# Relative bias tables: one slot and 32 writes, one per step, in place of three slots and 48 writes

## The chip, the cores and the metric

The kernel runs on one core of a Trainium2 chip. The time is device microseconds of one execution; before the change the median of three runs is 1170.31 us (1169.25 to 1171.8). The engines are named as in the profile: PE (TensorE matmul), PEld (its weight load), DVE (VectorE), ACT (ScalarE), POOL (GpSimd) and SP (the queue that issues most DMAs).

## What is computed

A two-layer encoder on 512 tokens (a grid of 8 rows and 64 columns) of width 1024, all in float32. Layer 0 is two kinds of global attention side by side, layer 1 a neighbourhood attention, and each is followed by a squared-ReLU MLP; a norm ends it. The change touches the bias of the neighbourhood attention, and the MLP of layer 0, beside which the bias is prepared:

```python
rs = jnp.clip(qr - wr // 2, 0, rows - wr)          # 8 rows of 8: always 0
cs = jnp.clip(qc - wc // 2, 0, GRID_W - wc)        # first of 16 columns
kr = rs[:, None, None] + jnp.arange(wr, dtype=jnp.int32)[None, :, None]
kc = cs[:, None, None] + jnp.arange(wc, dtype=jnp.int32)[None, None, :]
ridx = jnp.broadcast_to(kr - qr[:, None, None] + (C_WIN_ROWS - 1), (s, wr, wc)).reshape(s, -1)
cidx = jnp.broadcast_to(kc - qc[:, None, None] + (C_WIN_COLS - 1), (s, wr, wc)).reshape(s, -1)
...
bias = rpb[:, rblk, cblk].astype(jnp.float32)
sc = jnp.einsum('bhqd,bhqkd->bhqk', qblk, kg).astype(jnp.float32) * scale + bias[None]
...
def sq_relu_mlp(h, w_up, w_down):
    u = jax.nn.relu(h @ w_up)
    return (u * u) @ w_down
```

`rpb` has 16 heads, 15 row distances and 31 column distances.

## The kernel before

**Products in three passes.** Every float32 factor is split into a high part (fp32r, made by ACT) and a low part (the rest, made by DVE), and each product is three matmuls: high by high, high by low, low by high. `mm3` (L603 to L606) issues them for 512 columns, `Seven.run` (L448 to L450) for 256: the latter computes a 2 x 2 block product with seven products in place of eight, on sums of weight blocks that POOL forms (`seven_chunk`, L356 to L358) before ACT (L362, tile `whi`) and DVE (L363, tile `wlo`) split them.

**Memory.** SBUF holds 32 equal slots of 128 x 1024 floats. `Slot()` takes the one that has been free longest, `free()` puts it at the end of the list; whoever takes a slot waits for its last readers, DMAs included. Weights pass through `raw` (4 buffers), `whi` (3) and `wlo` (4).

**The second product of the MLP (`mlp(0)`).** It has three parts. First `product8` (L521 to L562): eight chunks of 128 rows of `ffn_w_down`, 512 KB each, against eight PSUM banks (s, t, t, o, mm, mm, mm, s), in 64 steps of three matmuls; the chunks k = 0 and 1 run first over four banks, then over the other four, k = 2 to 5 one after the other, and the last two bank by bank, so that DVE can add each bank into `hT` (L1536) as it is finished. From its third chunk on the low part of the weights is not made by DVE: SP loads the raw chunk (L252), ACT writes its negated high part to `wlo` (L255), a DMA that POOL issues (L256) adds the weights to it, and ACT makes the high part (L259). Second, beside these steps, `convert` splits the activations of the next product: ACT L417 and DVE L418, with DVE L390, L393 and L422 for the sums; each chunk takes new slots. Third, `u7.run` uses them, with weights of `seven_chunk` (SP L352). At its start another split takes two slots (ACT L964, DVE L961).

**The bias tables (`bias_rows`, L1472 to L1498).** For 16 column positions c within the window, and two kinds t of key sets (t = 0 for queries whose window lies inside, t = 1 for the tokens at the ends, whose other half is -1e30), the DRAM tensor `bx` receives a 128-row table of 256 values. Eight small DMAs (L1476) bring the bias, shifted by query row, into slot R; POOL fills slots Fi and Fe with -1e30 (L1479, L1480) and copies R into them (L1482, L1483); then SP writes, for each c, 128 KB from Fi (L1488), 64 KB from Fe (L1492) and 64 KB of -1e30 from Fe (L1494). It is a generator: `mlp` calls `next(bias)` twice per step of `product8` (L1560, L1561). In program order the writes fall on steps 7 to 30 of 64.

**The order on each engine.** A scheduler builds the rows of the engines from the program; what is marked `keep_in_program_order` stays in order, other work may be pulled forward. Each engine then runs its row in order. SP's DMAs use eight semaphores in turn, and each waits for the one eight places ahead.

**The reader.** In the neighbourhood attention each of the 16 heads loads its table from `bx` (L1789, 256 KB, two buffers `bias`), and DVE adds it to the scores (L1726). The same two buffers serve as split activations of the sixth chunk of `product8`.

Of the kernel before, what the change touches and what calls it, by code (L numbers as in the profile page):

```python
# [8 lines left out]
F32 = mybir.dt.float32  # L9
# [9 lines left out]
P = 128  # L19
# [3 lines left out]
NEG = -1e30  # L23
# [12 lines left out]
def encoder_kernel(ctx: ExitStack, tc: tile.TileContext, ins, out, dbg=None):  # L36
    nc = tc.nc
    PE, ACT, DVE, POOL, SP = nc.tensor, nc.scalar, nc.vector, nc.gpsimd, nc.sync
# [7 lines left out]
    dr = ctx.enter_context(tc.tile_pool(name="dr", bufs=1, space=bass.MemoryType.DRAM))  # L46
# [14 lines left out]
    def nm(s):  # L61
        cnt[0] += 1
        return f"{s}_{cnt[0]}"
# [271 lines left out]
    def finish_off():  # L335
        while off_d or off_a:
            catch_up()
# [30 lines left out]
    class Seven:  # L368
# [29 lines left out]
        def split(self, kp, held=lambda z: z):  # L398

            for b in range(7):  # L400
                i = self.number(kp, b) // 2
                if i not in self.slots:
                    self.slots[i] = Slot()
            raw, t = self.raw.pop(kp)
            own = isinstance(t, Slot)
            r, t_ = (s_.rearrange("p (b n) -> p b n", n=256) for s_ in (raw.t, t.t if own else t))

            T4 = t_[:, 2:3] if own else r[:, 3:4]
            src = lambda b, n: (r[:, 1 + b : 1 + b + n] if b < 3 else t_[:, b - 3 : b - 3 + n] if b < 5
                                else r[:, 0:1] if b == 5 else T4)  # L410
            b = 0
            while b < 7:
                q = self.number(kp, b)
                n = 2 if b == 3 or (b < 2 and q % 2 == 0) or (b == 5 and not own) else 1
                d = self.slots[q // 2].t.rearrange("p (q z n) -> p q z n", q=2, z=2)[:, q % 2 : q % 2 + n]
                s_ = r[:, 0:4:3] if b == 5 and n == 2 else src(b, n)
                ACT.activation(d[:, :, 0], s_, AF.Copy)  # L417
                held(DVE.tensor_tensor(d[:, :, 1], s_, f32(d[:, :, 0]), op=ALU.subtract))  # L418
                b += n
                yield  # L420
                if b == 3 and not own:
                    held(DVE.tensor_tensor(r[:, 3], r[:, 3], r[:, 0], op=ALU.subtract))  # L422
                    yield
            raw.free()
            if own:
                t.free()
# [140 lines left out]
    def tiles(c0, n):  # L567
        return [(c0 + o, min(P, n - o)) for o in range(0, n, P)]
# [5 lines left out]
    class Fill:  # L574
# [8 lines left out]
        def step(self):  # L583
            try:
                self.credit -= next(self.q[0][1])
            except StopIteration:
                self.q.pop(0)
# [879 lines left out]
        return stage, ahead, later  # L1467


    bx = dr.tile([16, 2, P, 256], F32, name="bx")  # L1470

    def bias_rows():  # L1472
        R, Fi, Fe = Slot(F32), Slot(F32), Slot(F32)
        rpb = ins["od_rpb"][0]
        for qr in range(8):
            SP.dma_start(R.t[16 * qr : 16 * qr + 16, 0:248],  # L1476
                           rpb.rearrange("h a b -> h (a b)")[:, (7 - qr) * 31 : (7 - qr) * 31 + 248])
            yield
        POOL.memset(Fi.t[:, 0:376], NEG)  # L1479
        POOL.memset(Fe.t[:, 256:512], NEG)  # L1480
        rv = R.t[:, 0:248].rearrange("p (k d) -> p d k", d=31)
        POOL.tensor_copy(Fi.t[:, 0:376].rearrange("p (j k) -> p j k", k=8)[:, 15:31, :], rv[:, 7:23, :])  # L1482
        POOL.tensor_copy(Fe.t[:, 0:248].rearrange("p (j k) -> p j k", k=8), rv)  # L1483
        for _ in range(6):
            yield
        bxv = bx.rearrange("h t (c r) k -> t c r h k", r=8)
        for c in range(16):
            SP.dma_start(bxv[0, c].rearrange("r h k -> r h k"), Fi.t[:, (15 - c) * 8 : (15 - c) * 8 + 256])  # L1488
            yield

            v, off = (1, (7 - c) * 8) if c < 8 else (0, (23 - c) * 8)
            SP.dma_start(bxv[1, c][:, :, 128 * v : 128 * v + 128], Fe.t[:, off : off + 128])  # L1492
            yield
            SP.dma_start(bxv[1, c][:, :, 128 - 128 * v : 256 - 128 * v], Fe.t[:, 256:384])  # L1494
            yield
        for s_ in (R, Fi, Fe):
            s_.free()
        yield  # L1498

    def convert(u7, R):  # L1500
        held = tc.keep_in_program_order
        for kp, raw in enumerate(R):
            yield from u7.sums(kp, raw, DVE, held)
            yield
            yield from u7.split(kp, held)

    def mlp(l, last=None):

        stage, ahead, later = first_product(l)
        reserve[0] = 3
        w = ins["ffn_w_down"][l]
        up4, gens4 = [], []

        def plain_last(k0, V):
            left = list(V)
            gens4.extend(product(w, k0, up4, tiles(512 * c, 512), lambda j, b, c=c: ev(4 * c + j, b), nk=2 * len(V))
                         for c in range(2))  # L1520

            def beside(m, i):
                if m == 0 and i % 8 == 4 and left:
                    w_ = left.pop(0)
                    for z in range(2):
                        U4.append(Slot())
                        up4.append(U4[-1].pair())
                        split(w_.t[:, S * z : S * z + S], up4[-1])
                    w_.free()

            return beside

        U4 = []

        def ev(m, b):
            return DVE.tensor_tensor(hT[:, m, :], hT[:, m, :], b, op=ALU.add)  # L1536

        U, _, _, (at_u, _), _ = stage(SIZES[l][0])
        up = [s_.pair() for s_ in U]
        gens = [product(w, at_u, up, tiles(512 * c, 512), lambda j, b, c=c: ev(4 * c + j, b)) for c in range(2)]  # L1540
        ahead()
        for c, gen in enumerate(gens):
            for i, _ in enumerate(gen):
                later(c, i)
        for s_ in U:
            s_.free()
        U, R, V, (at_u, at_r), late = stage(*SIZES[l][1:])
        first = [k + z for k in at_u for z in range(2)]
        gen = product8(w, first, U, ev)
        u7 = Seven(2 * len(R))  # L1550
        ids = [u7.plan(w, 256 * m, at_r) for m in range(4)]
        k0 = 32 - 2 * len(V)
        beside = (last or plain_last)(k0, V)
        bias = iter(()) if last else bias_rows()
        reserve[0] = NSLOT
        work, at = convert(u7, R), 0
        for i, _ in enumerate(gen):
            if i in (1, 4, 6):
                next(late, None)
            next(bias, None)  # L1560
            next(bias, None)  # L1561

            at += 9 * len(R) + 2
            while at > 0:
                next(work, None)
                at -= 8 * len(U) - 2
        for x in (work, bias):
            for _ in x:
                pass
        reserve[0] = 3  # L1570
        for m in range(4):

            def evac(w_):
                h2 = hT[:, 2 * m : 2 * m + 2, :]
                DVE.tensor_tensor(h2, h2, w_.t.rearrange("p (z n) -> p z n", z=2), op=ALU.add)

            for i, _ in enumerate(u7.run(ids[m], evac)):
                beside(m, i)
        u7.free()
        for gen in gens4:  # L1580
            for _ in gen:
                pass
        for s_ in U4:
            s_.free()
# [112 lines left out]
    def attend_C(step):  # L1697
# [45 lines left out]
        def weigh(w):  # L1743
            for p, tt in w:
                ACT.activation(p, p, AF.Exp, bias=tt[:, 0:1], scale=-1.0, accum_out=tt[:, 1:2])
# [35 lines left out]
        for n in range(16):  # L1781
            t, e = n // 2, n % 2
            if e == 0:
                fill.until(f"c{t}")
                finish_off()
            step(n)
            h = dict(d=PC[t], e=e, n=n)
            h["bias"] = scp.tile([P, 2, 256], F32, tag="bias", bufs=2, name=nm("bias"))
            SP.dma_start(h["bias"], bx[n].rearrange("t q k -> q t k"))  # L1789
            w = scores(h, (3, 0))  # L1790
            if prev:
                prev["pt"] = Slot(), Slot()
                turn(prev, *T1, w)
            else:
                weigh(w)
            rest(w, RATE_C - 0.15, ripe)
            w = scores(h, (1, 2))
            h["d"]["K"][e].free()
            if e:
                h["d"]["Q"].free()  # L1800
            if prev:
                turn(prev, *T2, w)
            else:
                weigh(w)
            rest(w, RATE_C + 0.15, None)
            prev, ripe = h, prev
# [265 lines left out]
```

## Time and profile before

| | |
|---|---|
| median of three runs | 1170.31 us (1169.25 to 1171.8) |
| profiled execution | 1171.35 us, its span 1169.6 us, mean granted clock 0.995 |
| PE, PEld busy | 98%, 88% |
| DVE, ACT, POOL busy | 76%, 57%, 51% |
| DMA | 134.37 MB, 115 GB/s |
| `product8` of layer 0 | 452 to 498 us of the span |

Times in the rows are microseconds from the span's start. A timeline row gives start, duration, engine, line, operation, output and input tiles, and in brackets how long the engine had been idle and what ended that. A row of windows gives a stretch, its length, the busy time of PE, PEld, DVE, ACT and POOL with the number of instructions, the granted TensorE clock (1.00 is full), the mean busy share of the core's 16 DMA engines, and GB/s. A row of a tile gives line, engine, operation, count, shortest, median and longest duration in ns, and the first and last start. Matmuls overlap, so their pace is read from their starts, not from their durations.

### The profile page before, as it was taken

What the parts mean: (1) busy time and instruction counts of PE and PEld (TensorE: products, weight loads), DVE (VectorE), ACT (ScalarE), POOL (GpSimd) and SP (SyncE); (2) the same over time, 40 slices, a digit from 0 to 9 for tenths busy, and PEclk for the clock granted to TensorE, in tenths of its full rate; (3) what the DMA queues carried; (4) which work ended last, traced back from release to release, by engine and by line L of the source; (5) the groups of instructions that cost most, each with busy time, mean ns of one, the idle gap of its engine ahead of it and who ended that gap; (6) DMA issues with size and microseconds to landing.
All of it is one profiled execution on the core that took longest, in us unless ns stands there. A gap on an engine that the chain in (4) does not pass through costs nothing.

```text
span 1169.6 us, 20581 instructions
## 1 busy us (share of the span) xinstructions
PE 1150.6 (98%) x7348; PEld 1025.9 (88%) x7348; DVE 892.6 (76%) x1544; ACT 668.4 (57%) x1135; POOL 602.0 (51%) x744
## 2 busy tenths in 40 slices
PE   9999999999999999989999999999999999999997
PEld 8787888887899999789987998988889999989996
DVE  6887988878868876676695676767997787688765
ACT  6676876756256658533453555655552666773445
POOL 4456252207687991279802232221288799526960
PEclk9999999999999999989999999999999999999999
DMA  7322314222523326823446564434343233282432
GB/s 234 108 75 66 96 59 131 64 84 91 168 77 88 100 73 180 221 82 100 127 127 160 135 176 133 125 102 136 99 148 105 83 99 99 60 202 64 127 118 72
DMA packets 115478, 134.37 MB, mean 115 GB/s; under 512 B 9667, under 2 KB 96880, under 8 KB 115376
## 3 DMA queue, kind: packets, MB, share of 16 engines
q1 hardware_dynamic: 111024, 120.09, 35.0%
q0 software_dynamic: 4032, 12.60, 5.5%
q8 instruction: 58, 0.95, 0.3%
q14 instruction: 44, 0.36, 0.1%
q10 hardware_dynamic: 320, 0.36, 0.1%
HBM read 110.61 MB, written 6.29 MB: 100 GB/s over the span
## 4 chain that ended last, share of the span: by engine, by line
PE 75%; DVE 7%; POOL 5%; DMA 4%; issue 4%; ACT 2%; SPq 2%; DVEq 0%; POOLq 0%; ACTq 0%
PE mm L604 8%; PE mm L605 8%; PE mm L606 8%; PE s L1128 3%; PE mm L450 3%; PE mm L448 3%; PE mm L449 3%; PE o L1116 3%; PE t L1103 2%; PE s L606 2%; PE s L604 2%; POOL raw L358 2%; PE s L605 2%; PE t L448 2%; PE t L450 2%
## 5 line engine op out<-in xcount | busy, mean ns | idle before, releaser
L604 PE MATMUL mm<-a,whi 128*128 128x512 f32 x428 | 173.8, 407 | 0.2
L363 DVE TENSOR_TENSOR wlo<-a,whi 128x896 fp32r<-128x896 f32 x103 | 130.1, 1266 | 53.8 <-ACT whi L362 53.5
L606 PE MATMUL mm<-a,wlo 128*128 128x512 f32 x428 | 168.9, 396 | 0.0
L605 PE MATMUL mm<-a,whi 128*128 128x512 f32 x428 | 168.9, 395 | 0.0
L362 ACT ACTIVATE whi<-a 128x896 fp32r<-128x896 f32 x103 | 97.5, 949 | 103.3 <-PE o L605 22.9
L233 ACT ACTIVATE whi<-raw 128x1024 fp32r<-128x1024 f32 (+3 forms) x100 | 92.2, 924 | 66.9 <-PE s L605 24.3
L223 DVE TENSOR_TENSOR wlo<-raw,whi 128x1024 fp32r<-128x1024 f32 (+4 forms) x97 | 110.0, 1138 | 25.1 <-ACT whi L233 20.8
L450 PE MATMUL mm<-a,wlo 128*128 128x256 f32 x430 | 120.7, 281 | 1.3 <-DVE wlo L363 1.2
L448 PE MATMUL mm<-a,whi 128*128 128x256 f32 x430 | 120.7, 281 | 0.0
L449 PE MATMUL mm<-a,whi 128*128 128x256 f32 x430 | 120.4, 280 | 0.0
L363 DVE TENSOR_TENSOR wlo<-raw,whi 128x896 fp32r<-128x896 f32 x61 | 72.8, 1197 | 49.8 <-ACT whi L362 49.5
L362 ACT ACTIVATE whi<-raw 128x896 fp32r<-128x896 f32 x61 | 57.9, 952 | 87.0 <-POOL raw L358 52.7
L358 POOL TENSOR_TENSOR a<-a 128x128 f32<-128x128 f32 x103 | 98.5, 956 | 8.1
L357 POOL TENSOR_TENSOR a<-a 128x256 f32<-128x256 f32 x103 | 94.9, 921 | 8.1
L606 PEld LDWEIGHTS mm<-a,wlo 128*128 128x128 f32 x428 | 80.3, 188 | 18.3
L604 PEld LDWEIGHTS mm<-a,whi 128*128 128x128 f32 x428 | 80.5, 188 | 17.1 <-issue 1.3
L605 PEld LDWEIGHTS mm<-a,whi 128*128 128x128 f32 x428 | 80.7, 189 | 14.9 <-DVE a L961 0.2
L1715 POOL TENSOR_SCALAR p<-p,ti 128x256 f32<-128x256 f32 x64 | 35.4, 563 | 105.5 <-DVE ti L1714 92.3
L448 PE MATMUL t<-a,whi 128*128 128x256 f32 x312 | 88.5, 284 | 1.2 <-DVE hT L1536 1.2
L1136 POOL TENSOR_SCALAR p<-p,ti 128x512 f32<-128x512 f32 x64 | 45.3, 708 | 86.0 <-DVE ti L1135 61.4
L449 PE MATMUL t<-a,whi 128*128 128x256 f32 x312 | 88.0, 282 | 0.0
L450 PE MATMUL t<-a,wlo 128*128 128x256 f32 x312 | 88.0, 282 | 0.0
(430 smaller groups left out, 3592.6 us busy)
## 6 DMA issues: line engine op xcount, KB each, us to landing
a<-in_ffn_w_up_dram SPq DMA_DIRECT2D x102, 256.0 KB
raw<-in_ffn_w_down_dram SPq DMA_DIRECT2D x34, 512.0 KB
raw<-in_ffn_w_down_dram SPq DMA_DIRECT2D x59, 256.0 KB
raw<-in_od_w_qkv_dram SPq DMA_DIRECT2D x64, 128.0 KB
raw<-in_ffn_w_up_dram SPq DMA_DIRECT2D x12, 512.0 KB
wlo<-in_ffn_w_down_dram POOLq DMA_DIRECT2D x12, 512.0 KB, 7.0
a<-a SPq DMA_DIRECT2D x18, 256.0 KB
bias<-bx SPq DMA_DIRECT2D x16, 256.0 KB
```

Of the source, the lines that this page charges most:

```text
L223: z = lambda: (eng or DVE).tensor_tensor(to, src, f32(high), op=ALU.subtract)
L233: ACT.activation(hi[:, 0:m], raw[:, 0:m], AF.Copy)
L357: held(POOL.tensor_tensor(r[:, 4:6], r[:, 2:3].to_broadcast([P, 2, P]), r[:, 0:7:6], op=ALU.add))
L358: held(POOL.tensor_tensor(r[:, 7], r[:, 3], r[:, 5], op=ALU.subtract))
L362: ACT.activation(hi[:, 0:896], raw[:, 128:1024], AF.Copy)
L363: DVE.tensor_tensor(lo[:, 0:896], raw[:, 128:1024], f32(hi[:, 0:896]), op=ALU.subtract)
L448: PE.matmul(o, wh, x[:, 0], start=kp == 0 and n in (0, 1, 3, 5), stop=False, skip_group_check=True)
L449: PE.matmul(o, wh, x[:, 1], start=False, stop=False, skip_group_check=True)
L450: PE.matmul(o, wl, x[:, 0], start=False, stop=kp == self.np - 1, skip_group_check=True)
L604: PE.matmul(o, wh, xh, start=first, stop=False)
L605: PE.matmul(o, wh, xl, start=False, stop=False)
L606: PE.matmul(o, wl, xh, start=False, stop=last)
```

## The change

Three slots become two: R, and F, which holds Fi in its first 376 columns and Fe in the other 648. One memset fills F with -1e30; Fe's bias copy moves to its columns 128 to 375, so that -1e30 stands on both sides of it. R is freed after the copies instead of at the end. `bx` is laid out as [2, 128, 16, 256] in place of [16, 2, 128, 256]: the rows of one c are contiguous for all heads. So the write from Fi has 128 rows of 1 KB, and the two writes of t = 1 become one, which reads two runs of 128 values from F (one with the bias, one of -1e30) for each row. `next(bias)` is called once per step: in program order the 32 writes fall on steps 14 to 45. The reading DMA takes rows 16 KB apart.

```diff
-    bx = dr.tile([16, 2, P, 256], F32, name="bx")
+    bx = dr.tile([2, P, 16, 256], F32, name="bx")
 
     def bias_rows():
-        R, Fi, Fe = Slot(F32), Slot(F32), Slot(F32)
+
+        R, F = Slot(F32), Slot(F32)
+        Fi, Fe = F.t[:, 0:376], F.t[:, 376:1024]
         rpb = ins["od_rpb"][0]
...
-        POOL.memset(Fi.t[:, 0:376], NEG)
-        POOL.memset(Fe.t[:, 256:512], NEG)
+        POOL.memset(F.t, NEG)
         rv = R.t[:, 0:248].rearrange("p (k d) -> p d k", d=31)
-        POOL.tensor_copy(Fi.t[:, 0:376].rearrange("p (j k) -> p j k", k=8)[:, 15:31, :], rv[:, 7:23, :])
-        POOL.tensor_copy(Fe.t[:, 0:248].rearrange("p (j k) -> p j k", k=8), rv)
+        POOL.tensor_copy(Fi.rearrange("p (j k) -> p j k", k=8)[:, 15:31, :], rv[:, 7:23, :])
+        POOL.tensor_copy(Fe[:, 128:376].rearrange("p (j k) -> p j k", k=8), rv)
+        R.free()
         for _ in range(6):
             yield
-        bxv = bx.rearrange("h t (c r) k -> t c r h k", r=8)
+        bxv = bx.rearrange("t (c r) h k -> t c (r h) k", r=8)
         for c in range(16):
-            SP.dma_start(bxv[0, c].rearrange("r h k -> r h k"), Fi.t[:, (15 - c) * 8 : (15 - c) * 8 + 256])
+            SP.dma_start(bxv[0, c], Fi[:, (15 - c) * 8 : (15 - c) * 8 + 256])
             yield
 
-            v, off = (1, (7 - c) * 8) if c < 8 else (0, (23 - c) * 8)
-            SP.dma_start(bxv[1, c][:, :, 128 * v : 128 * v + 128], Fe.t[:, off : off + 128])
+            at, step = (0, 128 + (7 - c) * 8) if c < 8 else (128 + (23 - c) * 8, 248 - (23 - c) * 8)
+            two = Fe[:, at : at + 2 * step].rearrange("p (z n) -> p z n", z=2)[:, :, 0:128]
+            SP.dma_start(bxv[1, c].rearrange("q (z n) -> q z n", z=2), two)
             yield
-            SP.dma_start(bxv[1, c][:, :, 128 - 128 * v : 256 - 128 * v], Fe.t[:, 256:384])
-            yield
-        for s_ in (R, Fi, Fe):
-            s_.free()
+        F.free()
         yield
...
             next(bias, None)
-            next(bias, None)
...
-            SP.dma_start(h["bias"], bx[n].rearrange("t q k -> q t k"))
+            SP.dma_start(h["bias"], bx[:, :, n].rearrange("t q k -> q t k"))
```

In the changed kernel the lines are: bias loads L1478, memset L1481, copies L1483 and L1484, writes L1490 (from Fi) and L1495 (from Fe), reading DMA L1788. Other lines keep their numbers up to L1557. The rows of PE are the same, and those of the other engines differ only around `product8` of layer 0.

## The prediction

> **What bounds the kernel now.** I began with the page: engine shares, then the chain that ended last.
>
> ```profile
> PE 1150.6 (98%) x7348; PEld 1025.9 (88%) x7348; DVE 892.6 (76%) x1544; ACT 668.4 (57%) x1135; POOL 602.0 (51%) x744
> PE 75%; DVE 7%; POOL 5%; DMA 4%; issue 4%; ACT 2%; SPq 2%; DVEq 0%; POOLq 0%; ACTq 0%
> ```
>
> TensorE is busy 98% of the span, so an edit that touches no matmul can win only where PE waits or its clock falls. The busy time by stretches says where that is.
>
> ```profile
> 440.00:510.00 70.00, 64.82 (x334) 54.97 (x333) 51.50 (x83) 41.73 (x62) 18.32 (x24) 0.95 0.67 175
> 510.00:620.00 110.00, 108.28 (x830) 103.33 (x829) 77.66 (x99) 47.36 (x61) 67.16 (x81) 1.00 0.39 116
> 620.00:790.00 170.00, 169.41 (x1038) 149.84 (x1037) 109.50 (x300) 91.45 (x215) 47.98 (x90) 1.00 0.53 140
> ```
>
> Columns: length, busy time of PE, PEld, DVE, ACT, POOL, granted clock, DMA share, GB/s. The table writes fall into 440 to 510 us, which holds 5.2 us of PE idle time and a mean clock of 0.95. The stretch that reads the tables, 620 to 790, has 0.6 us of idle. So the PE rows of the first stretch:
>
> ```profile
> 485.19 0.39 PE L604 MATMUL s<-p,whi 128*128 128x512 f32 x1
> ...
> 486.10 0.39 PE L605 MATMUL s<-p,whi 128*128 128x512 f32 x1
> 487.92 0.50 PE L606 MATMUL s<-p,wlo 128*128 128x512 f32 x1 [1.43 <-DMA wlo<-in_ffn_w_down_dram]
> ...
> 497.57 0.39 PE L606 MATMUL s<-p,wlo 128*128 128x512 f32 x1
> 500.39 0.36 PE L448 MATMUL s<-a,whi 128*128 128x256 f32 x1 [2.43 <-DVE hT L1536]
> ...
> 510.34 0.28 PE L448 MATMUL s<-a,whi 128*128 128x256 f32 x1
> ...
> 511.97 0.28 PE L450 MATMUL t<-a,wlo 128*128 128x256 f32 x1
> ```
>
> The 48 matmuls (8 banks, 2 chunks, 3 each) that end the eight-bank product start from 485.19 to 497.57. At the undisturbed spacing of 0.227 us (485.19 to 486.10 is four) the last would start at 495.86. **Loss 1.71.** The next, at 500.39, is 2.82 later instead of 0.23. **Loss 2.59.** From there two chunks of 21 matmuls take 9.95 us, to 510.34; at the spacing behind it (14 in 1.63 us, 0.1164) they need 4.89. **Loss 5.06**, because the clock fell:
>
> ```profile
> 500.00:502.00 2.00, 1.03 (x6) 0.85 (x7) 2.00 (x5) 0.12 (x1) 1.84 (x3) 1.00 0.16 54
> 502.00:504.00 2.00, 1.40 (x8) 1.11 (x7) 2.00 (x3) 2.00 (x3) 1.84 (x4) 0.53 0.00 0
> 504.00:506.00 2.00, 1.98 (x9) 1.69 (x9) 2.00 (x4) 0.20 (x1) 0.71 (x1) 0.50 0.04 8
> 506.00:508.00 2.00, 1.87 (x9) 1.58 (x8) 2.00 (x4) 0.95 (x1) 0.00 (x0) 0.50 0.00 0
> 508.00:510.00 2.00, 2.00 (x15) 2.00 (x14) 2.00 (x4) 0.00 (x0) 0.00 (x0) 0.76 0.42 131
> ```
>
> The missing shares of the last four rows are 2 x (0.47+0.50+0.50+0.24) = 3.4 us of full clock; the rest of 5.06 is waiting for L1536. Together 9.36 us. Who is late? The first loss waits for a weight DMA, the second for VectorE's evacuation (L1536). Their sources:
>
> ```profile
> 479.63 1.06 ACT L255 ACTIVATE wlo<-raw 128x1024 fp32r<-128x1024 f32 x1 [3.29 <-DMA raw<-in_ffn_w_down_dram]
> 480.99 0.86 POOL L256 DMA_DIRECT2D wlo<-in_ffn_w_down_dram  x1 [8.39 <-DMA bx<-a]
> 493.29 0.63 ACT L417 ACTIVATE a<-sc 128x512 fp32r<-128x512 f32 x1 [6.75 <-DMA bx<-a]
> 481.25 0.69 DVE L418 TENSOR_TENSOR a<-a,a 128x512 fp32r<-128x512 f32 x1 [4.06 <-ACT a L417]
> 493.95 0.69 DVE L418 TENSOR_TENSOR a<-sc,a 128x512 fp32r<-128x512 f32 x1 [4.47 <-DMA bx<-a]
> 499.57 0.67 DVE L1536 TENSOR_TENSOR hT<-hT,s 128x512 f32<-128x512 f32 x1
> ```
>
> POOL's wait is put down to a table write, but L255 ended at 480.69, just before it, so it waited for ScalarE and that for the raw chunk. ACT and DVE at 493 wait for slots Fi and Fe, which the conversion takes again and the table writes still read. DVE stands 4.47 us, then works without a gap to the evacuation that PE awaits. Both come from one stream, SP's:
>
> ```profile
> 455.02 2.18 SPq L1494 DMA_DIRECT2D bx<-a  x1
> 459.30 1.33 SPq L252 DMA_DIRECT2D raw<-in_ffn_w_down_dram  x3
> 468.37 0.80 SPq L252 DMA_DIRECT2D raw<-in_ffn_w_down_dram  x1
> 490.71 0.57 SPq L1494 DMA_DIRECT2D bx<-a  x1
> ```
>
> The three L252 loads stand behind the writes, one of which SP needed 2.18 us to issue; the last chunk's raw load, issued at 468.37, had landed only at 479.6 (L255 above); the last write went out at 490.71.
>
> **The change part by part.** *How fast the writes go.* The bytes stay: 32 x 128 KB = 4.19 MB. The shape does not: 8x16x256 and 8x16x128 become 128x256 and 256x1x128.
>
> ```profile
> 472.00:474.00 2.00, 2.00 (x10) 1.61 (x9) 1.87 (x4) 0.64 (x1) 0.60 (x1) 1.00 1.05 250
> 488.00:490.00 2.00, 2.00 (x9) 1.66 (x10) 1.48 (x4) 0.00 (x0) 0.00 (x0) 1.00 0.56 182
> 490.00:492.00 2.00, 2.00 (x11) 1.65 (x10) 0.00 (x0) 0.00 (x0) 0.00 (x0) 1.00 0.56 178
> L1488 SPq DMA_DIRECT2D bx<-a x16: 570/600/980, 443.6 to 489.5; - x16
> L1789 SPq DMA_DIRECT2D bias<-bx x16: 366/370/633, 494.1 to 779.8; - x16
> ```
>
> From 488 to 492 SP issues table writes back to back and the 16 DMA engines are busy 0.56; mixed with weight loads they reach 1.05. I read the old writes as using half of the engines: 180 GB/s at 0.56 would be 180/0.56 = 321 GB/s on all. The stream then needs 4.19 MB/321 GB/s = 13.1 us instead of 4.19/180 = 23.3. Issue: L1789, whose outer size is 128, takes 0.37 us against 0.57 to 0.60. With the 0.04 between rows, 32 x 0.41 = 13 us instead of 48 x 0.61 = 29. Bounds: at worst the shape matters nothing and the last write lands near 493.9 as now; at best it is only behind what precedes it in SP's row.
>
> [...]
>
> *SP's row.* It starts alike: 17 writes stand ahead of the three L252 loads in both. Its end, at the last writes: before, then changed.
>
> ```order
> L1488 DMA bx_3041<-a_1056_5410 8x16x256
> L1492 DMA bx_3041<-a_1057_5411 8x16x128
> L1494 DMA bx_3041<-a_1057_5411 8x16x128
> L352 DMA raw_1090_5664<-in_ffn_w_down_dram 128x2x256
> L352 DMA raw_1097_5718<-in_ffn_w_down_dram 128x2x256
> L352 DMA raw_1105_5768<-in_ffn_w_down_dram 128x2x256
> L1789 DMA bias_1308_7303<-bx_3041 128x2x256
> ```
>
> ```order
> L1495 DMA bx_3041<-a_1056_5410 256x1x128
> L1490 DMA bx_3041<-a_1056_5410 128x256
> L352 DMA raw_1081_5574<-in_ffn_w_down_dram 128x2x256
> L1495 DMA bx_3041<-a_1056_5410 256x1x128
> L352 DMA raw_1089_5632<-in_ffn_w_down_dram 128x2x256
> L352 DMA raw_1096_5694<-in_ffn_w_down_dram 128x2x256
> L352 DMA raw_1104_5750<-in_ffn_w_down_dram 128x2x256
> L1788 DMA bias_1307_7285<-bx_3041 128x2x256
> ```
>
> One write stands behind raw_1081, the product's successor's first load, where 14 stood before. raw_1081 needs the buffer that an L259 frees:
>
> ```profile
> 466.47 1.04 ACT L259 ACTIVATE whi<-raw 128x1024 fp32r<-128x1024 f32 x1
> 475.30 1.04 ACT L259 ACTIVATE whi<-raw 128x1024 fp32r<-128x1024 f32 x1
> 491.89 2.88 DMA raw<-in_ffn_w_down_dram
> ```
>
> That ends at 467.5 or earlier; 0.4 for the issue and 2.9 to land (the raw load at 491.89) put the last write at about **470 to 471**. I take this, since 13 us of writes end before it even beside the loads.
>
> *The slot.* F returns late to the free list and goes to a_1120, the first split after the product, which the scheduler pulled forward on ACT. Before, around the last two chunks, then changed:
>
> ```order
> L259 ACTIVATE whi_1092_5675<-raw_1063_5442 128x1024
> L255 ACTIVATE wlo_1091_5666<-raw_1074_5534 128x1024
> L417 ACTIVATE a_1089_5648<-a_973_4864 128x2x256
> L417 ACTIVATE a_1109_5788<-a_1024_5260 128x2x256
> L417 ACTIVATE a_1095_5698<-sc_1093_5685 128x2x256
> L259 ACTIVATE whi_1098_5723<-raw_1074_5534 128x1024
> L417 ACTIVATE a_1096_5699<-a_990_4996 128x2x256
> L964 ACTIVATE a_1121_5882<-a_1033_5364 128x512
> L417 ACTIVATE a_1102_5739<-sc_1099_5728 128x2x256
> ```
>
> ```order
> L417 ACTIVATE a_1100_5717<-a_1024_5260 128x256
> L964 ACTIVATE a_1120_5864<-a_1033_5364 128x512
> L417 ACTIVATE a_1087_5615<-sc_1084_5598 128x2x256
> L259 ACTIVATE whi_1091_5643<-raw_1062_5437 128x1024
> L255 ACTIVATE wlo_1090_5634<-raw_1073_5516 128x1024
> ```
>
> The wait for all writes moves from a_1102 (Fi) and a_1103 (Fe) to L964, now ahead of L259 and L255 of the last chunks; DVE's L961 moved likewise. ACT reaches it about 474: the L259 behind it stands at 475.30 now, where PE frees its buffer. That is 3 us after the writes landed, so it costs nothing.
>
> *What comes free.* raw_1073 no longer sits 11 us in the queues, so L255 runs about 476 instead of 479.63. POOL's DMA then lands within the present 6.9 us (480.99 to 487.92) at 484, before PE's need at 486.33: **1.71 goes**. DVE loses neither 4.47 nor most of 4.06 (it waited for ACT, and ACT for that raw load), so its first evacuation comes near 492 instead of 499.57, against PE's need at 496.1 (495.86 and 0.23): **2.59 goes**, and with the gap the clock loss: **5.06 goes**. What is late next: the second and third chunk's L362 wait for weight buffers that PE frees only at 496, then L363; I charge 0.5.
>
> *The rest.* The memset grows to 1024 columns:
>
> ```profile
> 439.37 0.42 POOL L1479 MEMSET a<- 128x376 f32 x1 [1.23 <-DVE wlo L363]
> 443.13 0.43 POOL L1482 COPY a<-a 128x128 f32<-128x128 f32 x1 [3.35 <-DMA a<-in_od_rpb_dram]
> 728.96 0.63 SPq L1789 DMA_DIRECT2D bias<-bx  x1
> 740.35 0.42 DVE L1726 CUSTOM_DVE_ANT_0 p<-s,bias 128x256 f32<-128x256 f32 x1
> ```
>
> 0.42 x 1024/376 = 1.1 us ends at 440.5, covered by the wait for the bias load to 443.13; uncovered it would be 0.7. The table reads are now 1 KB rows 16 KB apart: each is issued some 11 us ahead (728.96 for 740.35), against about 3 to land, so it would need to be almost four times slower to show: zero.
>
> **Sum.** 9.4 - 0.5 = 8.9 us. The profiled execution, 1171.35 (span 1169.6 and 1.75 around it), becomes 1162.4. It lies 1.04 above the median of the runs, 1170.31, so the median becomes 1161.4.
>
> **Rivals.** *Forecast*, 1160 to 1164: chance 0.70.
>
> *Slower: L964 stops ACT.* Mechanism: the last write lands at T, later than ACT's arrival; L964, L417, L259, L255 take about 3.2 us (0.6+0.6+1+1), POOL's start 0.3, landing 6.9, so wlo is there at T + 10.4. PE waits from T = 475.9. If T stays 493.9, PE waits 18, less the 9.4, plus a clock drop like the present one (3.4 lost): 1170.3 + 12 = 1182. Slower than now from T = 482. [...] Against: 0.56 and the 13 us. Chance 0.09.
>
> *Half the gain.* Writes speed up, but DVE stays behind at the start of the next product: it must gain 3.5 us (499.57 to 496.1) of 8.5 now waited. If ACT holds it up, only 1.7 and part of the 2.59 go and the clock still drops: 1164 to 1168. Chance 0.16.
>
> *No gain.* The next product's chunks pass POOL one by one; if POOL cannot start earlier, PE runs dry once the ready chunks are used, and its gain is lost there.
>
> ```profile
> 510.07 1.25 POOL L356 TENSOR_TENSOR raw<-raw 128x128 f32<-128x128 f32 x1 [5.35 <-DVE wlo L363]
> ```
>
> POOL resumes at 510.07 only because it waited 5.35 for DVE, which is earlier too. 1168 to 1172, chance 0.05.
>
> **How the numbers follow.** The 0.70 and 0.16 reach from 1159.5 to 1168 and hold about 0.84; 0.09 above and the no-gain case are left out. 0.2% (2.3 us) is about what a measurement of this kernel tells from no change: faster 0.86, same 0.05, slower 0.09.
>
> **What would show it.** DMA share above 0.9 while table writes run; the last L1495 issued before 470; ACT's L964 without a DMA wait over 1 us; no PE wait at L606 for wlo; the first L448 within 0.5 us of the last L606; clock 1.00 throughout. A wait of ACT L964 on bx of several us, or a table write still running at 480, would prove me wrong.

## The result, and the profile after

The changed kernel takes 1171.87 us (median of 12 runs, 1170.07 to 1172.92); the kernel before, on the same chip beside it, 1169.94 (12 runs). The ratio is 1.0012 with a 95% interval of 1.0003 to 1.0021. The forecast was 1161.4, with a range from 1159.5 to 1168: the gain of 8.9 us did not come. The profiled span is 1170.2 us, against 1169.6.

The busy time by stretches of the changed kernel (length, then PE, PEld, DVE, ACT and POOL busy, granted clock, DMA share, GB/s):

```profile
440.00:510.00 70.00, 63.98 (x333) 53.86 (x332) 51.68 (x82) 41.40 (x61) 18.99 (x24) 0.95 0.65 174
510.00:620.00 110.00, 107.76 (x826) 102.70 (x825) 77.62 (x99) 47.36 (x61) 67.12 (x81) 1.00 0.39 116
620.00:790.00 170.00, 169.34 (x1039) 149.81 (x1038) 109.54 (x299) 91.40 (x215) 47.98 (x90) 1.00 0.53 140
```

The stretch with the table writes still has 6.0 us of idle PE (5.2 before) and a clock of 0.95. The stretch that reads the tables is as it was. So the same size of loss stands in the same 70 us, and the question is whether it is the same loss. The PE rows of the changed kernel, with the idle time ahead of each and what ended it in brackets:

```profile
484.88 0.39 PE L604 MATMUL s<-p,whi 128*128 128x512 f32 x1
...
489.64 0.79 PE L604 MATMUL s<-p,whi 128*128 128x512 f32 x1 [3.90 <-ACT whi L259]
...
491.28 0.79 PE L606 MATMUL s<-p,wlo 128*128 128x512 f32 x1 [0.42 <-DMA wlo<-in_ffn_w_down_dram]
...
502.65 0.39 PE L606 MATMUL s<-p,wlo 128*128 128x512 f32 x1
502.88 0.28 PE L448 MATMUL s<-a,whi 128*128 128x256 f32 x1
...
505.74 0.39 PE L448 MATMUL o<-a,whi 128*128 128x256 f32 x1 [0.71 <-DVE hT L1536]
...
507.94 0.38 PE L450 MATMUL s<-a,wlo 128*128 128x256 f32 x1 [0.98 <-DVE wlo L363]
```

It is not the same. The wait at the start of the next product is gone: L448 follows L606 by 0.23 us, where 2.82 stood. The wait for wlo shrank from 1.43 to 0.42. In their place PE waits 3.90 us for the last chunk's whi, which did not wait before. Then the clock falls, in the 2 us stretches of the changed kernel:

```profile
476.00:478.00 2.00, 2.00 (x10) 1.62 (x9) 0.00 (x0) 0.00 (x0) 0.00 (x0) 1.00 1.13 270
478.00:480.00 2.00, 2.00 (x10) 1.62 (x9) 0.00 (x0) 0.00 (x0) 0.00 (x0) 1.00 1.03 260
480.00:482.00 2.00, 2.00 (x11) 1.65 (x10) 0.00 (x0) 0.00 (x0) 0.00 (x0) 1.00 0.69 232
482.00:484.00 2.00, 2.00 (x11) 1.65 (x10) 0.78 (x2) 1.44 (x3) 0.00 (x0) 1.00 0.02 8
...
488.00:490.00 2.00, 0.36 (x1) 0.36 (x2) 1.99 (x3) 1.58 (x2) 1.84 (x4) 0.54 0.96 180
490.00:492.00 2.00, 1.58 (x4) 0.76 (x4) 1.97 (x4) 0.63 (x1) 1.92 (x3) 0.50 0.87 248
492.00:494.00 2.00, 2.00 (x6) 1.52 (x5) 2.00 (x3) 0.00 (x0) 1.84 (x3) 0.50 0.62 203
```

The 48 matmuls that end the product run from 484.88 to 502.65. Undisturbed (47 steps of 0.227 us) the last would start at 495.55, so 7.1 us are lost there, and 0.71 and 0.98 behind: 8.8 us, against 9.36 before. The 0.6 us between the two are lost again from 510 to 620, where PE is busy 107.76 us in place of 108.28.

The first rows also point at the cause. From 476 to 482 DVE, ACT and POOL do nothing at all, while the DMA engines work at shares of 1.13, 1.03 and 0.69; when the share falls to 0.02, ACT and DVE start, and POOL after them. ACT, POOL and DVE of the changed kernel:

```profile
472.84 1.23 ACT L417 ACTIVATE a<-a 128x512 fp32r<-128x512 f32 x3
482.56 0.63 ACT L964 ACTIVATE a<-a 128x512 fp32r<-128x512 f32 x1 [8.49 <-DMA bx<-a]
483.09 0.62 ACT L417 ACTIVATE a<-sc 128x512 fp32r<-128x512 f32 x1
483.62 1.05 ACT L259 ACTIVATE whi<-raw 128x1024 fp32r<-128x1024 f32 x1
484.57 1.04 ACT L255 ACTIVATE wlo<-raw 128x1024 fp32r<-128x1024 f32 x1
...
488.54 1.04 ACT L259 ACTIVATE whi<-raw 128x1024 fp32r<-128x1024 f32 x1
```

```profile
485.90 0.86 POOL L256 DMA_DIRECT2D wlo<-in_ffn_w_down_dram  x1 [12.76 <-ACT wlo L255]
```

```profile
483.22 0.69 DVE L961 TENSOR_TENSOR a<-a,a 128x512 fp32r<-128x512 f32 x1 [8.44 <-ACT a L964]
...
500.58 0.68 DVE L1536 TENSOR_TENSOR hT<-hT,s 128x512 f32<-128x512 f32 x1
```

ACT is ready at 474.07 and stands 8.49 us at L964, which writes into the tables' buffer F, until the last table write has landed. Everything queued behind it on ACT is late: L255 at 484.57 (479.63 before), so POOL's L256 at 485.90 (480.99), and the last L259 at 488.54, for which PE waits. DVE stands as long, 8.44 us, at L961, which needs what L964 writes. Its first evacuation L1536 comes at 500.58, no earlier than the 499.57 of before; PE does not wait for it at the start of the next product only because PE itself comes 5 us later. This is the rival that the prediction calls "L964 stops ACT".

### The profile page after: what moved, and what is told of

Read it like the earlier page. It is cut to its first block, busy times and chain, and to the rows that moved or that the text cites. A ratio compares the mean times of both kernels' runs of the same rounds, so it can differ in the third digit from the quotient of the medians.

```text
span 1170.2 us, 20549 instructions
## 1 busy us (share of the span) xinstructions
PE 1150.1 (98%) x7348; PEld 1025.0 (88%) x7348; DVE 892.2 (76%) x1544; ACT 668.5 (57%) x1135; POOL 602.9 (52%) x743
## 4 chain that ended last, share of the span: by engine, by line
PE 79%; DVE 6%; POOL 5%; DMA 4%; issue 3%; ACT 1%; SPq 1%; DVEq 0%; POOLq 0%; ACTq 0%
PE mm L604 8%; PE mm L605 8%; PE mm L606 8%; PE s L1128 3%; PE mm L450 3%; PE mm L448 3%; PE mm L449 3%; PE o L1116 3%; PE t L1103 2%; PE t L450 2%; PE t L448 2%; PE t L449 2%; PE s L606 2%; PE s L604 2%; PE s L605 2%
## 5 line engine op out<-in xcount | busy, mean ns | idle before, releaser
L606 PE MATMUL mm<-a,wlo 128*128 128x512 f32 x428 | 169.1, 396 | 0.0
L448 PE MATMUL mm<-a,whi 128*128 128x256 f32 x430 | 120.8, 281 | 0.0
L606 PEld LDWEIGHTS mm<-a,wlo 128*128 128x128 f32 x428 | 80.4, 188 | 18.2
L448 PE MATMUL t<-a,whi 128*128 128x256 f32 x312 | 87.8, 281 | 0.0
```

The source lines that it names most:

```text
L448: PE.matmul(o, wh, x[:, 0], start=kp == 0 and n in (0, 1, 3, 5), stop=False, skip_group_check=True)
L606: PE.matmul(o, wl, xh, start=False, stop=last)
```

## The experiments

**Theory A**: L964's place in ACT's row, ahead of the last weight conversions, is the whole loss; with it out of the way the faster writes bring most of the forecast. **Theory B**: the DMA engines are full from 450 to 482 us, so the last weight loads are late whoever holds the buffer. The changed kernel in that stretch:

```profile
450.00:482.00 32.00, 32.00 (x148) 26.34 (x147) 19.73 (x35) 20.08 (x33) 3.39 (x4) 1.00 1.02 270
```

In each comparison the kernel before ran on the same chip: 1170.63 us beside e1, e2, e3 and e5; 1170.77 beside e6, e7, e9 and e10; 1171.73 beside e11, f14, f18 and f22.

### Keep the buffer: e1_hold_F

```diff
-        F.free()
+        kept.append(F)
...
             for i, _ in enumerate(u7.run(ids[m], evac)):
                 beside(m, i)
+            while m == 1 and kept:
+                kept.pop().free()
```

> The changed kernel with F's buffer kept until the second block of the next product, so that no early instruction of ACT or DVE takes it while the table writes still read it. Theory A (the changed kernel lost its gain only because ACT's L964 took F's buffer and stood 8.5 us for the last write, to 482.6 us): no wait on a table write on ACT or DVE; the last chunk's L255 no longer at 484.6 but near 476 to 479; the 3.9 us wait of PE for L259 and the clock of 0.54 and 0.50 behind it go; 3.9 + 3.4 us and most of the two small waits come back: 1161 to 1163 us, ratio about 0.992. Theory B (the DMA engines are full from 450 to 481 us, share 1.00 to 1.16, so the last raw loads are late whoever holds the buffer): raw loads still land after 478, PE waits 2 to 4 us at L604 or L606, 1167 to 1171 us.

Measured: 1164.51 us, ratio 0.9947 (0.9934 to 0.9959). ACT in this kernel:

```profile
474.62 1.05 ACT L259 ACTIVATE whi<-raw 128x1024 fp32r<-128x1024 f32 x1
476.09 1.06 ACT L255 ACTIVATE wlo<-raw 128x1024 fp32r<-128x1024 f32 x1 [0.42 <-DMA raw<-in_ffn_w_down_dram]
...
479.57 1.04 ACT L259 ACTIVATE whi<-raw 128x1024 fp32r<-128x1024 f32 x1
```

The last raw load is there at 476, although the engines still carry the same transfers (a share of 1.02 to 1.15 from 476 to 484), and the last L259 runs 9 us earlier. Theory B falls here. The time is 1.5 us above the range that A named.

### Only the layout: e2_shape_only

The kernel before, with three buffers and 48 writes, but 128 rows in each write:

```diff
-    bx = dr.tile([16, 2, P, 256], F32, name="bx")
+    bx = dr.tile([2, P, 16, 256], F32, name="bx")
...
-        bxv = bx.rearrange("h t (c r) k -> t c r h k", r=8)
+        bxv = bx.rearrange("t (c r) h k -> t c (r h) k", r=8)
...
-            SP.dma_start(bxv[1, c][:, :, 128 * v : 128 * v + 128], Fe.t[:, off : off + 128])
+            SP.dma_start(bxv[1, c][:, 128 * v : 128 * v + 128], Fe.t[:, off : off + 128])
...
-            SP.dma_start(h["bias"], bx[n].rearrange("t q k -> q t k"))
+            SP.dma_start(h["bias"], bx[:, :, n].rearrange("t q k -> q t k"))
```

> The kernel before with only the new layout of bx (2 x 128 x 16 x 256, so that each write has 128 rows): three buffers, 48 writes, two per step of the product, and ACT's and DVE's order as before. Theory A: the last write lands near 482 instead of 494; the waits of L417 and L418 for Fi and Fe at 493 shrink to nothing, since ACT reaches them only near 486; the first evacuation L1536 is in time and the clock stays 1.00: 1161 to 1164 us. If only part of DVE's lateness goes, 1164 to 1167. Theory B: DMA share above 1.0 until the writes end and the last raw loads as late as now (L255 at 479.6 or later), 1168 to 1171 us.

Measured: 1162.07 us, ratio 0.9929 (0.9916 to 0.9941), the fastest of all. Its first stage and the wait for the old buffer Fi:

```profile
440.00:510.00 70.00, 70.00 (x414) 61.93 (x413) 56.36 (x87) 44.80 (x65) 27.40 (x36) 1.00 0.72 192
```

```profile
483.94 0.64 ACT L417 ACTIVATE a<-sc 128x512 fp32r<-128x512 f32 x1 [1.84 <-DMA bx<-a]
```

PE has no idle time from 440 to 510 and the clock stays 1.00. The wait for Fi at 493.29 (6.75 us) has become 1.84 us at 483.94, where nothing urgent stands behind it. So the new shape alone brings the gain that was forecast for the whole change, although its table writes land no earlier than the 482.5 of the changed kernel.

### Only the place: e9_hold_place

```diff
-        ACT.activation(dst[:, 0, :], src, AF.Copy)
+        held(ACT.activation(dst[:, 0, :], src, AF.Copy))
...
-                        split(w_.t[:, S * z : S * z + S], up4[-1])
+                        split(w_.t[:, S * z : S * z + S], up4[-1], held=tc.keep_in_program_order)
```

L964 still takes F; it only stays where the program writes it, 15 rows further back on ACT, beside the other L964, which moves too. Both L961 that follow them on DVE move back as well; the rows of PE, POOL and SP are those of the changed kernel.

> The changed kernel with one thing undone: the L964 that takes F's buffer (and its twin) is held at the place where the program writes it, behind the last L259 and L255 of the eight-bank product; buffer, writes and their pacing stay. Theory A (only the place of L964 in ACT's row costs): ACT no longer stands at L964, the last L255 runs at 476 to 478, PE no longer waits 3.9 us and its clock stays 1.00; DVE also has two L961 (0.6 us each) less before the product's end than the kernel that kept F: 1160 to 1164 us. Theory B (full DMA engines make the last loads late): PE still waits 2 us or more and 1167 us or more. If something else had gone wrong with the single buffer, it would stay near 1170 too.

Measured: 1164.07 us, ratio 0.9944 (0.9931 to 0.9956).

```profile
440.00:510.00 70.00, 69.72 (x407) 61.07 (x406) 58.16 (x86) 44.13 (x64) 27.25 (x32) 1.00 0.69 189
510.00:620.00 110.00, 107.62 (x790) 101.03 (x789) 76.33 (x100) 47.20 (x62) 61.61 (x77) 1.00 0.40 121
```

Buffer, writes and pace are those of the changed kernel, the DMA engines as full (share 1.06 from 450 to 482), and the first stage's loss is gone: from 6.0 us idle to 0.3, with the clock at 1.00. This is the most direct test of A: the place of L964, with L961 behind it, is the loss (the two were not moved apart). The time lies at the upper edge of A's range, 0.07 us above it. In the next 110 us PE idles 2.4 us, 0.7 more than in the kernel before.

### Two writes per step, and the old shape: e3_two_per_step, e5_old_layout

```diff
             next(bias, None)
+            next(bias, None)
```

> The changed kernel with two writes issued per step of the product, as before. F comes free earlier in the program and goes to an L417 that stands further ahead on ACT, reached near 469 us, ahead of every L259 and L255 of the last chunks. Theory A (the cost is ACT standing at the taker of F until the last write): ACT stands 8 to 12 us from about 469, the last weight chunks are later than in the changed kernel, PE waits more than 4 us: slower, 1174 to 1182 us. Theory B (the cost is the full DMA engines, the same work in the same stretch): about as the changed kernel, 1170 to 1173 us.

Measured: 1175.11 us, ratio 1.0034 (1.0022 to 1.0047). F is freed earlier in the program and another instruction takes it, still further ahead on ACT:

```profile
470.31 0.63 ACT L417 ACTIVATE a<-a 128x512 fp32r<-128x512 f32 x1 [0.76 <-DVE a L418]
479.09 0.42 ACT L417 ACTIVATE a<-a 128x256 fp32r<-128x256 f32 x1 [8.15 <-DMA raw<-in_ffn_w_down_dram]
479.41 1.04 ACT L259 ACTIVATE whi<-raw 128x1024 fp32r<-128x1024 f32 x1
```

The profile puts the 8.15 us down to a raw load, but L417 here reads no raw chunk; the DMAs that the program has it wait for are the last table writes, which read F. (The same holds below where F's taker is said to wait for a raw load.) The writes landed 3.5 us earlier than in the changed kernel, and it is slower: what counts is what stands behind the wait.

```diff
-    bx = dr.tile([2, P, 16, 256], F32, name="bx")
+    bx = dr.tile([16, 2, P, 256], F32, name="bx")
...
-            SP.dma_start(bxv[1, c].rearrange("q (z n) -> q z n", z=2), two)
+            for z in range(2):
+                SP.dma_start(bxv[1, c][:, :, 128 * z : 128 * z + 128], two[:, z])
```

> The changed kernel with the old layout of bx and three DMAs per table pair, so 48 writes of the shapes 8x16x256 and 8x16x128, still from one buffer and on one step of pacing each pair. The writes go on half of the DMA engines as before (share 0.56 where they run alone), the last lands near 490 to 495. Theory A: ACT stands at L964 until then, some 10 us longer than in the changed kernel, and with it the last L259: PE waits 8 to 14 us and loses 3 to 4 us of clock: 1176 to 1186 us. Theory B (it matters how full the engines are, not who holds the buffer): less crowded DMA engines, so the raw loads are no later, 1168 to 1173 us.

Measured: 1178.55 us, ratio 1.0066 (1.0051 to 1.0081).

```profile
493.31 0.63 ACT L964 ACTIVATE a<-a 128x512 fp32r<-128x512 f32 x1 [14.42 <-DMA raw<-in_ffn_w_down_dram]
```

```profile
495.98 0.80 PE L604 MATMUL s<-p,whi 128*128 128x512 f32 x1 [10.79 <-ACT whi L259]
```

With the old shape the last write lands at 493.3, as in the kernel before (493.29), and PE waits 10.79 us instead of 3.90. L964 stood some rows further back here (behind the last L255, still ahead of the last L259), so the price is not the shape's alone. The landing time is the shape's: 10.8 us later than in the changed kernel, and e2_shape_only, also with 48 writes but of the new shape, had Fi's near 483.9.

### Where the buffer comes free: e11, f14, f18, f22

Three buffers in place of two (R too is kept to the end), the 32 writes, their shape and their pace as in the changed kernel:

```diff
-        R, F = Slot(F32), Slot(F32)
-        Fi, Fe = F.t[:, 0:376], F.t[:, 376:1024]
+        R, F, G = Slot(F32), Slot(F32), Slot(F32)
+        Fi, Fe = F.t[:, 0:376], G.t[:, 376:1024]
...
-        F.free()
+        for s_ in (R, F, G):
+            s_.free()
```

> The changed kernel with three buffers again, freed together after the last write as before; 32 writes, one per step, new layout. If the single buffer itself cost the gain, it is at 1161 to 1164 us. If only the place in the program at which a buffer comes free counts (it stays after step 46, so L964 takes one again and stands at the same place or three rows further ahead on ACT, before the last L259 and L255), it stands there until the last write at about 482, PE waits some 4 us: 1170 to 1174 us. The latter is what I expect.

Measured: 1173.16 us, ratio 1.0012 (1.0002 to 1.0022).

```profile
482.24 0.63 ACT L964 ACTIVATE a<-a 128x512 fp32r<-128x512 f32 x1 [8.17 <-DMA raw<-in_ffn_w_down_dram]
```

PE then waits 3.4 us for L259: the picture of the changed kernel. Merging the buffers is not the cause.

The other three change only the pace, in one place, with 14, 18 or 22 for N. In the program F is then freed at step 30, 32 or 34, two steps apart, and not four as I wrote for 18:

```diff
             next(bias, None)
+            if i >= N:
+                next(bias, None)
```

> The changed kernel with two writes per step from step 14 on, so that F's buffer comes free near step 30, as in the kernel before; one buffer, 32 writes. F then goes to an L417 that stands on ACT four rows behind the last L259, which ACT reaches near 483 to 486. Theory (the place decides): no wait on a write over 1 us, or one that ends before 484, PE and clock undisturbed: 1161 to 1164.5 us. Rival (the pace or the full DMA engines decide): 1167 us or more.

> The same with two writes per step from step 18 on. F comes free four steps later and goes to another L417, which the scheduler put ahead of the last L259, L255 and L259 on ACT, reached near 471 to 475. Theory: ACT stands there until the last write at 480 to 482 and PE waits 3 to 5 us: 1169 to 1174 us, though the writes hardly differ from those of the kernel with two from step 14. Rival (pace or DMA load decides): the same time as that kernel, within 1.5 us.

> The same with two writes per step from step 22 on. F comes free near step 34 and goes to an L417 seven rows behind the last L259 on ACT, reached near 488. Theory: nothing waits for a write, PE and clock undisturbed: 1161 to 1164.5 us. Rival (later is worse): between the kernel with two from step 18 and the changed kernel, 1169 to 1173 us.

Measured: 1165.08 us, 0.9944 (0.9931 to 0.9956), for 14; 1172.33, 1.0006 (0.9997 to 1.0015), for 18; 1164.85, 0.9942 (0.9929 to 0.9956), for 22. 14 and 22 came out 0.6 and 0.4 us above what I expected, 18 within it. The stretch from 440 to 510 with 22, then ACT and PE with 18:

```profile
440.00:510.00 70.00, 69.29 (x404) 60.81 (x403) 56.88 (x86) 44.12 (x64) 26.67 (x33) 1.00 0.70 189
```

```profile
481.12 0.63 ACT L417 ACTIVATE a<-a 128x512 fp32r<-128x512 f32 x1 [7.69 <-DMA raw<-in_ffn_w_down_dram]
```

```profile
488.08 0.50 PE L604 MATMUL s<-p,whi 128*128 128x512 f32 x1 [2.61 <-ACT whi L259]
...
489.90 0.79 PE L606 MATMUL s<-p,wlo 128*128 128x512 f32 x1 [1.07 <-DMA wlo<-in_ffn_w_down_dram]
```

The last writes are issued at 473.3, 472.1 and 470.6 us: hardly different, and in one order, while the time goes down, up and down again with the place of F's taker on ACT (behind, ahead of and again behind the last L259). Neither pace nor DMA load can do that.

### What sets the landing time: e7_plain_load

```diff
-        tc.keep_in_program_order(POOL.dma_start(v(lo_), src, accum_op=ALU.add))
+        tc.keep_in_program_order(POOL.dma_start(v(lo_), src))
```

> The changed kernel with POOL's accumulating DMA (L256) turned into a plain load of the same bytes, so that the low halves of the weights are wrong in this product: it changes part of the computation. Packets of 4 KB took 330 to 350 ns with accumulation and 160 to 190 ns as plain loads; over 443 to 483 us the accumulating ones hold 14 of some 36 us of work on each of the 16 engines. Theory: the last table write lands when all this work is done, so T moves from 482.4 to about 475 to 477, ACT's wait at L964 falls from 8.5 to 2 to 4 us, PE's wait for L259 goes: 1161 to 1165 us. Rival (T is set by the pace at which SP issues the writes, one pair a step): T stays at 480 or later, ACT waits 6 us or more, 1168 to 1172 us.

This kernel leaves out the addition of the weights to their negated high part: `wlo` holds the whole weights. The bytes and the matmuls stay.

Measured: 1166.81 us, ratio 0.9964 (0.9951 to 0.9978). The DMA queues from 443 to 483 us (kind: packets, MB, share of 16 engines), of the changed kernel and of this one; q0 carries POOL's DMAs, q1 SP's:

```profile
q1 hardware_dynamic: 7661, 7.33, 56.2%
q0 software_dynamic: 720, 2.62, 35.0%
```

```profile
q1 hardware_dynamic: 7923, 7.55, 58.0%
q0 software_dynamic: 838, 3.09, 24.1%
```

```profile
476.73 0.63 ACT L964 ACTIVATE a<-a 128x512 fp32r<-128x512 f32 x1 [4.73 <-DMA bx<-a]
```

With accumulation 2.62 MB took 35.0% of 40 us, 14.0 us or 5.3 us per MB; without, 3.09 MB took 9.6 us, 3.1 per MB. That is 5.8 us less for 2.62 MB, and L964 ran at 476.73 instead of 482.56: 5.8 us earlier. So one write per step does not hold the landing at 482; the other work on the engines moves it. The last write was also issued earlier, at 468.94 instead of 475.88, so this run does not tell a full engine from a late issue. The time came out above the 1161 to 1165 that I expected: ACT still stood 4.73 us, and DVE's L1536 was late for PE three times (0.51, 0.57 and 0.70 us).

### Two that tried for more: e6_hold_F_two, e10_early_writes

The kernel that kept F, with a second `next(bias, None)` per step:

```diff
             next(bias, None)
+            next(bias, None)
```

> The kernel that kept F's buffer (1164.5 us), with two writes per step in place of one. It asks whether that kernel's 2.4 us above the three-buffer one (1162.1) come from later writes: then the raw loads behind the writes come some 3 us earlier and it reaches 1162 to 1163 us. If they come from the order of DVE's work at the end of the product (two L961 ahead of the last L363 and evacuations, DVE busy without a gap from 484 to 502), it stays at 1164 to 1165 us.

Measured: 1164.45 us, ratio 0.9951 (0.9935 to 0.9968): the pace makes no difference when nobody waits for the buffer. The other reading, by the order of DVE's work, is not proved by that, and e9 speaks against it: there both L961 run behind the evacuations, and the time is 1164.07. Why e2_shape_only is 1.5 to 2.6 us faster, by the ratios, than all the others in which nobody waits for the tables stays open; the intervals of e2 and of each of these overlap.

The table build begun two products earlier:

```diff
                 for u, _ in enumerate(x7.run(ids, (pair_evac, raw_evac)[kind])):
                     if u in (14, 21, 24):
                         next(state["late"], None)
+                    if tick and i >= len(kinds) - 2:
+                        tick()
...
+        def tick():
+            if not made:
+                made.append(bias_rows())
+            next(made[0], None)
...
-        bias = iter(()) if last else bias_rows()
+        bias = iter(()) if last else made[0]
```

> The changed kernel with the table build and its 32 writes begun two products earlier, in the stretch up to 440 us where the DMA share is 0.12 to 0.36, so that no table write is left between 445 and 483. If the full DMA engines of 450 to 481 cost nothing that a later place of L964 does not also save, it equals the kernel with the place held: 1160 to 1164 us. If the crowded engines cost something of their own, it is 1 to 3 us below that one. If the two buffers it takes from the earlier products make their loads late, there are new PE waits before 440 and it lies at 1164 to 1168 us.

Measured: 1172.74 us, ratio 1.0019 (1.0010 to 1.0028): no gain, a miss for each of the expectations. In this kernel:

```profile
461.91 0.96 POOL L256 DMA_DIRECT2D wlo<-in_ffn_w_down_dram  x1 [23.51 <-ACT wlo L255]
```

```profile
469.55 0.79 PE L606 MATMUL s<-a,wlo 128*128 128x512 f32 x1 [5.32 <-DMA wlo<-in_ffn_w_down_dram]
```

All 32 writes now stand in SP's row ahead of the six L252 loads, which go out only from 456.51 (the changed kernel issued its first at 441.91). POOL's first accumulation starts at 461.91 instead of 448.03, and PE waits 5.32 us in the middle of the product and then runs at a clock of 0.50 from 470 to 472. The same loss again, from a third place. The DMA-light stretch was hardly reached: the writes went out from 436.06 to 455.89.

## Why the prediction was wrong, step by step

**The step that failed** is the landing of the last write: "I take this, since 13 us of writes end before it even beside the loads", with 470 to 471 us. It was 482.5. SP's last rows in the changed kernel:

```profile
475.45 0.38 SPq L352 DMA_DIRECT2D raw<-in_ffn_w_down_dram  x1
475.88 0.97 SPq L1495 DMA_DIRECT2D bx<-a  x1
```

The last write went out at 475.88, where I had it at 467.5, and landed 6.7 us later instead of 3.3 (0.4 and 2.9). From the first issue at 443.39 to the last are 32.5 us in place of 13. Two terms were too small.

One is SP's issue. The 0.37 us came from loads that stand alone in SP's row. In e10 SP issues table writes back to back, with next to nothing else on the DMA engines:

```profile
441.00:452.00 11.00, 11.00 (x94) 10.95 (x93) 5.41 (x8) 9.40 (x17) 0.00 (x0) 1.00 0.65 204
```

```profile
L1492 SPq DMA_DIRECT2D bx<-a x16: 320/606/610, 436.1 to 455.2; - x16
L1497 SPq DMA_DIRECT2D bx<-a x16: 439/525/1694, 436.6 to 455.9; - x16
```

Most took 0.52 to 0.62 us, as the old writes did, and the 32 went out from 436.06 to 455.89: 19.8 us, though the engines had room (a share of 0.65). The 13 us hold up as engine time alone: in these 11 us 2.24 MB (204 GB/s) kept the engines at 0.65, 7.15 us, which is 13.4 us for 4.19 MB.

The other is what the same 16 engines do beside the writes. From 443 to 483 us SP's queue worked 56.2% of 40 us, 22.5 us, for 7.33 MB; the writes' share by bytes is 12.9, so 9.6 are raw loads and the rest, and POOL's accumulations come to 14.0. Together that is 36.5 us of work; with the engines full from the first write at 443.4 it would end at 479.9. I had a row for it: a DMA share of 1.05 at 472 to 474, against 0.56 where the old writes ran alone, meant that other transfers took up the rest. e7 bears this out: taking 5.8 us of work away moved the landing by 5.8. How much later the issue alone would have made it stays open.

**"That is 3 us after the writes landed, so it costs nothing"** fell with it. ACT's arrival was right (about 474; it was 474.07), the order of arrivals was not. The rival had the mechanism, its place and its break-even: slower than before from a landing at 482; the landing was 482.5 and the ratio 1.0012. It priced the wait by `wlo`, while PE's longer wait was for `whi` (3.90 us, then 0.42 for `wlo`). I gave it 0.09, because I held the margin of 3 us for safe without bounding the landing from above by the work beside it. The range of that time, 470 to 494, lay on both sides of ACT's arrival, so its bounds should have stood in the chances.

**The forecast for DVE**, "its first evacuation comes near 492", failed in the changed kernel too, for the same reason: DVE stood at L961 behind L964, and L1536 ran at 500.58. With L964 and L961 moved back (e9) it is as forecast:

```profile
491.39 0.67 DVE L1536 TENSOR_TENSOR hT<-hT,s 128x512 f32<-128x512 f32 x1
```

**Right.** The new writes use more of the engines: table writes alone reached a share of 0.72 in e10 (450 to 452 us), where the old ones stood at 0.56. The landing times of e5 and the changed kernel, 493.3 and 482.5, agree with that. Half of the engines for the old writes and all of them, at 321 GB/s, for the new ones was my estimate from the 0.56; no run shows how many engines carried a write, and in e10 the table writes moved 228 GB/s at the 0.72. The memset, 0.96 us, was hidden by the wait for the bias load (2.92 us behind it). The table reads cost nothing (169.34 busy, 169.41 before).

**The size of the gain.** With L964 out of the way the losses named in the prediction do come back: e9 has 4.9 us more of PE busy time from 440 to 510 and the 3.4 us of clock, less 0.7 and 0.2 in the two stretches behind: 7.4, and its profiled execution (1163.96) lies 7.4 below that of the kernel before (1171.35); by the medians it is 6.7. The forecast had 8.9. I had charged 0.5 for what would be late next; by these rows it was 1.2 (0.3, 0.7 and 0.2). And the loss of 9.36, read from starts, is 8.6 by idle time and clock (5.2 and 3.4).

## What to carry to other kernels

Freeing a buffer is an edit of the schedule: who takes it next, and what stands behind that instruction on its engine, decided some 7 us here, and moving the release by two steps at a time switched it on and off again. Before an added wait is costed at nothing, bound the time of its releaser by all the work on that resource, the neighbours' too, and take issue times from rows that stand back to back. When a transfer is moved ahead in a queue, look at what it is moved past.

## What the runs showed of the hardware

- From 443 to 483 us POOL's DMAs that accumulate into `wlo` kept the engines 5.3 us per MB in the changed kernel, its plain loads 3.1 in e7.
- The new shape did not make SP's issue faster back to back: 0.52 to 0.62 us for most writes in e10 at a DMA share of 0.65, as the old 0.57 to 0.60. After a pause a write from Fi took 0.32 to 0.35 (e10 at 436.06 and 450.63, the changed kernel at 443.39, 466.58 and 473.34). Between 449 and 457 us of the changed kernel, at a DMA share of 0.99, some writes took up to 1.62; one of e10, at 445.34, took 1.69 (a share of 0.35 from 446 to 448). In the changed kernel (ns, minimum, median, maximum), where 570/600/980 stood:

```profile
L1490 SPq DMA_DIRECT2D bx<-a x16: 328/634/1616, 443.4 to 473.3; - x16
```

- The clock fell to 0.50 behind a PE wait of 2.61 us that ended at 488.08 (f18: 1.00 until 488, 0.67 from 488 to 490, 0.50 from 490 to 494), and it stayed 1.00 behind one of 1.34 (e1).
